# Mean squares of the heads summed along the free axis, the last square sum on VectorE, and the first normalisation dealt out anew over three engines

## The chip, the cores and the metric

The kernel runs on one core of a Trainium2 chip. The core has five engines with their own instruction queues: TensorE (PE; its weight loads are listed apart as PEld), VectorE (DVE), ScalarE (ACT), GpSimd (POOL) and SyncE (SP), which here only issues DMAs. The metric is the device time of one execution in microseconds; the median of several runs counts. Everything is FP32 in and out.

## The reference, cut to what matters

One layer of an encoder on 512 tokens of 1024 channels:

```python
h = rms_norm(x, norm1_g)                      # mean of squares over the 1024 channels
proj = h @ w_in                               # pool, attention, recurrence, gates
y_attn: o = (softmax(s1) - lam * softmax(s2)) @ v        # 4 heads of 128 channels
        o = rms_norm(o, gain) * 0.8                      # over the 128 channels of a head
y_rec:  o = o_forward + o_backward                       # 4 heads of 128 channels
        o = rms_norm(o, gain) * silu(g)
merged = sum of gate * (y @ w_up); x = x + merged @ w_out
x = x + (silu(h2 @ w_a) * (h2 @ w_b)) @ w_ffn_out        # h2 = rms_norm(x, norm2_g)
return rms_norm(x, final_norm_g)
```

So there are eight head norms over 128 channels each (four of attention, four of the recurrence), a first norm, a second norm and a final norm over 1024 channels.

## The kernel before

**Layout.** Most activations lie transposed: channels on the 128 partitions, the 512 tokens along the free axis (four blocks of 128, `NB = 4`). A product is made exact enough by splitting both sides into a rounded part and a remainder (`_hi`, `_lo`, type FP32R) and adding three products hi x hi, hi x lo, lo x hi. ScalarE makes the rounded part of a weight (`whi`, L191), VectorE the remainder (`wlo`, L192), 128x1024 at a time. Small products inside the heads are plain FP32.

**Order of the work.** TensorE's order is the program's: `mm` (L96) and `transpose` (L104) pin it. It is made when the kernel is built, by a small planner (`Pipe`): heads and a stream of weight jobs are Python generators; each `yield ("w", t, slack)` says that the head's next piece should stand at least t us of planned TensorE time later, with up to `slack` of putting off so that small pieces of several heads come together; `yield ("e", name, t)` waits for a named event. The other engines' order is set by the framework from a simulated timeline, except where the program pins one instruction behind another (`behind`, `issue_after`). Every queue runs in order, so an instruction that waits holds up those behind it on its engine.

**Head norms** (`head_norm`, L692 to L717). A head's output is in PSUM, 128 channels by 512 tokens. ScalarE squares it (`sqo`, L697) and copies it times the gain (`og`, L698). TensorE sums over the partitions by four FP32 products with `onesD` (a column of 1/128), one per token block: the result is a 128x4 tile, tokens on the partitions. VectorE adds epsilon (for attention it first multiplies twice by the softmax denominators' reciprocal `rr`), GpSimd takes the power -1/2 (`rso`, L147), and TensorE spreads the result again over the channels by four transposes of a broadcast column. VectorE then multiplies `og` with it. In the recurrence `og` is also multiplied with the silu gate (L1013, L1014); `rec_scan` and `att_head` call the helper at L1011 and L1158.

**Front** (L558 to L689, written out by hand). The blocks of x arrive by SyncE's queue in the order x, x, weights rq, weights rf, x, x, weights rb. For each of four token blocks `norm_rows` squares 1024 columns on ScalarE with an accumulated sum, GpSimd adds epsilon and takes the power, VectorE makes two 512-wide products with the row factor and the gain (which stands spread over the partitions in two PSUM banks, `g_ps`; for blocks 2 and 3 ScalarE first copies it to `g_b`). `rows_T` transposes the rows on TensorE, ScalarE casts the result (`hT_hi`, L515), VectorE makes its remainder (`hT_lo`, L519). Eleven products of no use (`probe`) keep TensorE running before that. Then three weight tiles take their first products with token blocks 0 and 1 (`turns`), the transposes of blocks 2 and 3 between them.

**Tail** (`seven_job`, the last of the output products). Token blocks 2 and 3 come last. For the last block ScalarE squares columns 512 to 1023, 0 to 255 and 256 to 511 into three accumulators (`out_sums`, L1479), VectorE adds the three (`out_rstd`, L1495), GpSimd takes the power, ScalarE scales one half of the columns and VectorE the other, and each half is stored by the queue of ScalarE or of SyncE (`out_store`, L1503 to L1506).

Of the kernel before, what the change touches and what calls it, by code (L numbers as in the profile page):

```python
# [11 lines left out]
F32 = mybir.dt.float32  # L12
# [6 lines left out]
P = 128  # L19
# [63 lines left out]
def encoder_kernel(ctx: ExitStack, tc: tile.TileContext, x, norm1_g, w_in, pool_w, pool_scale,  # L83
# [48 lines left out]
    onesD, minus1 = fixed[:, 0:1], fixed[:, 1:2]  # L132
    nc.vector.memset(onesD, 1.0 / P)
# [15 lines left out]
    def rsqrt_eps(dst, mean):  # L149

        ms = small.tile([P, 8], F32, name="ms")[:, :mean.shape[1]]
        eng = nc.vector if mean.space == PSUM else nc.gpsimd
        eng.tensor_scalar(out=ms, in0=mean, scalar1=1.0, scalar2=EPS, op0=ALU.mult, op1=ALU.add)  # L153
        return pow_mhalf(dst, ms)
# [335 lines left out]
    def norm_rows(src, g_b, work, after=()):  # L490
        sq = work.tile([P, D], F32, name="hrow")
        ss = small.tile([P, 1], F32, name="ss")
        with behind(after):
            on_act = nc.scalar.activation(out=sq, in_=src, func=AF.Square, scale=D ** -0.5, accum_out=ss).ins
        rstd = small.tile([P, 1], F32, name="rstd")
        rsqrt_eps(rstd, ss)
        h = work.tile([P, D], F32, name="hrow")
        for half in range(2):
            cs = slice(half * 512, half * 512 + 512)
            g = g_b[half] if isinstance(g_b, list) else g_b[:, cs]  # L500
            with behind(after):
                on_dve = nc.vector.scalar_tensor_tensor(out=h[:, cs], in0=src[:, cs], scalar=rstd, in1=g,  # L502
                                                        op0=ALU.mult, op1=ALU.mult).ins
        return h, on_dve, on_act
# [44 lines left out]
    g_b = xg.tile([P, D], F32, name="g1b")  # L549
# [9 lines left out]
    for name in ("x", "x", "rq", "rf", "x", "x", "rb"):  # L559
        if name == "x":  # L560
            t, src = xp.tile([P, D], F32, name="xin"), xblk[len(xt)]
            xt.append(t)
# [32 lines left out]
    nc.vector.tensor_copy(out=g_cols, in_=gt[:, 0:KT])  # L595
# [10 lines left out]
    for _ in range(11):  # L606
# [7 lines left out]
    def first_split(after):  # L614
        f = First()
        with behind(after):
            f.hi, f.lo = split_w(first_raw[len(first)], KT, P, None, 64)
        first.append(f)
        return LAST["whi"], LAST["wlo"]

    h0, on_dve, on_act = norm_rows(xt[0], g_ps, xw)
    h1, on_dve, on_act = norm_rows(xt[1], g_ps, xw, (on_act, on_dve))
    last = first_split((on_act, on_dve))
    for h, b, where in ((h0, 0, ("tp", "tp")), (h1, 1, ("rc", "mm"))):
        for half in range(2):
            with behind(last):
                on_act = rows_T(h, hT, b, half, None, where[half])
            last = on_act, LAST["hT_lo"]
    on_act, on_dve = first_split(last)
    for half in range(2):  # L630
        with tc.issue_after(on_act):
            on_act = nc.scalar.copy(out=g_b[:, half * 512:half * 512 + 512], in_=g_ps[half]).ins
    last = on_act, on_dve
    h2, on_dve, on_act = norm_rows(xt[2], g_b, xw, last)
    h3, on_dve, on_act = norm_rows(xt[3], g_b, xw, (on_act, on_dve))
    last = first_split((on_act, on_dve))
# [44 lines left out]
    turns(0, 4)  # L681
    turns(1, 8)
# [9 lines left out]
    def head_norm(o_ps, tmp, gain, r0=None, bufs=2, slack=0.0):  # L692
# [3 lines left out]
        sq = tmp.tile([P, S], F32, name="sqo", bufs=bufs)  # L696
        nc.scalar.activation(out=sq, in_=o_ps, func=AF.Square)  # L697
        nc.scalar.activation(out=og, in_=o_ps, func=AF.Copy, scale=gain)  # L698
        yield ("w", 1.3, slack)
        sp = bank("tp")  # L700
# [1196 lines left out]
```

## Time and profile before

| what | value |
|---|---|
| median of 3 runs | 871.75 us (871.43 to 872.48) |
| the profiled execution's own time | 871.81 us |
| its span, first to last instruction | 870.0 us |
| busy: TensorE, VectorE, ScalarE, GpSimd | 862.4, 659.2, 448.7, 37.1 us |
| DMA | 87.54 MB, 101 GB/s in the mean |

A timeline row gives start, length, engine, line, operation, output<-inputs, shapes, and how many like instructions follow each other; in brackets stands how long the engine had been idle before and what ended that. A row of a tile's or a line's instructions gives shortest, median and longest duration in ns and the first and last start in us. A row of windows gives the stretch, then for TensorE, its weight loads, VectorE, ScalarE and GpSimd the busy us and the number of instructions, then the granted clock, the DMA share and GB/s. A page row of waits gives the waiting engine and line, what it waited for, and total, number and longest in us.

### The profile page before, as it was taken

Reading aid. Unit: us, or ns where it says so; the run is one execution under the profiler, and the core shown is the slowest. Engines: PE = TensorE matmul, PEld = TensorE weight load, DVE = VectorE, ACT = ScalarE, POOL = GpSimd, SP = SyncE. Lnnn points to the kernel's source line nnn. Section 1 sums busy time; section 2 is a strip of 40 time slices with the busy share of each in tenths; the row PEclk is TensorE's granted clock in tenths of the full one; section 3 lists DMA queues with packets and bytes.
Section 4 is the critical chain, followed back from the end, with each engine's and each line's share of the span. In section 5 each row is a group of like instructions: output and inputs, shape, how many; then the busy total and the mean of one; then the engine's idle time right before and its main releaser. Section 6 shows DMA issues by size and latency. Waiting matters only on the chain.

```text
span 870.0 us, 14113 instructions
## 1 busy us (share of the span) xinstructions
PE 862.4 (99%) x5713; PEld 786.1 (90%) x5713; DVE 659.2 (76%) x979; ACT 448.7 (52%) x721; POOL 37.1 (4%) x83
## 2 busy tenths in 40 slices
PE   9999999999999999999999999999999999999997
PEld 8989998888988888899999998999999999988886
DVE  6779644845757888987776756988888888847996
ACT  6644343435757664563354425655555655533563
POOL 2000000000102220000000001000000000000001
PEclk9999999999999999999999999999999999999999
DMA  8330113024133321343332840344433433355002
GB/s 245 98 122 25 50 49 121 25 74 151 43 95 90 90 68 49 97 146 98 97 98 97 288 124 1 85 112 128 114 98 108 136 98 99 121 194 192 2 1 98
DMA packets 115694, 87.54 MB, mean 101 GB/s; under 512 B 3862, under 2 KB 104748, under 8 KB 115628
## 3 DMA queue, kind: packets, MB, share of 16 engines
q1 hardware_dynamic: 115036, 85.57, 32.2%
q8 instruction: 45, 0.74, 0.4%
q10 hardware_dynamic: 592, 1.05, 0.3%
q14 instruction: 21, 0.17, 0.1%
HBM read 84.52 MB, written 2.10 MB: 100 GB/s over the span
## 4 chain that ended last, share of the span: by engine, by line
PE 98%; issue 1%; DMA 0%; DVE 0%; POOL 0%; ACT 0%; POOLq 0%
PE mm L96 65%; PE rc L96 28%; PE tp L96 3%; PE tp L104 2%; DMA xin<-in_x_dram 0%; PE rc L104 0%; DVE hrow L502 0%; POOL rstd L147 0%; ACT silu L1479 0%; ACT x L1503 0%; DVE x L1472 0%; DVE x L1481 0%; PE mm L104 0%; POOLq L1892 0%; POOL ms L153 0%
## 5 line engine op out<-in xcount | busy, mean ns | idle before, releaser
L191 ACT CAST whi<-raw 128x1024 fp32r<-128x1024 f32 (+1 forms) x134 | 127.5, 959 | 140.7 <-PE mm L96 95.2
L192 DVE TENSOR_TENSOR wlo<-raw,whi 128x1024 fp32r<-128x1024 f32 (+1 forms) x134 | 147.8, 1106 | 50.9 <-ACT whi L191 41.3
L96 PE MATMUL mm<-hT_hi,whi 128*128 128x512 f32 (+1 forms) x344 | 81.3, 370 | 0.0
L96 PE MATMUL mm<-hT_hi,wlo 128*128 128x512 f32 (+1 forms) x344 | 80.0, 368 | 0.0
L96 PE MATMUL mm<-hT_lo,whi 128*128 128x512 f32 (+1 forms) x344 | 78.8, 367 | 0.0
L96 PEld LDWEIGHTS mm<-hT_hi,whi 128*128 128x128 f32 x344 | 59.2, 188 | 10.3 <-ACT hT_hi L515 0.2
L96 PEld LDWEIGHTS mm<-hT_lo,whi 128*128 128x128 f32 x344 | 59.1, 188 | 9.8
L96 PEld LDWEIGHTS mm<-hT_hi,wlo 128*128 128x128 f32 x344 | 58.8, 188 | 9.5
L318 DVE TENSOR_TENSOR slo<-sums,shi 128x1024 fp32r<-128x1024 f32 x54 | 65.7, 1217 | 0.0
L316 ACT CAST shi<-sums 128x1024 fp32r<-128x1024 f32 x54 | 56.8, 1052 | 4.1 <-DVE sums L280 3.3
L276 DVE TENSOR_TENSOR sums<-raw 128x1024 f32<-128x1024 f32 x27 | 32.9, 1218 | 1.2 <-DMA raw<-in_w_in_dram 1.2
L96 PE MATMUL mm<-y_arena,whi 128*128 128x512 f32 x128 | 32.7, 394 | 0.0
L96 PE MATMUL mm<-whi,y_arena 128*128 128x256 f32 (+1 forms) x192 | 32.1, 317 | 0.0
L96 PE MATMUL rc<-kq,kc 128*128 128x128 f32 x224 | 30.4, 284 | 0.0
L96 PEld LDWEIGHTS rc<-kq,kc 128*128 128x128 f32 x224 | 29.2, 191 | 1.1
L961 DVE TENSOR_TENSOR kq<-kq,pyr 128x256 f32<-128x256 f32 x48 | 18.2, 420 | 15.8 <-PE rc L96 15.8
L96 PEld LDWEIGHTS mm<-whi,y_arena 128*128 128x128 f32 x192 | 27.9, 189 | 2.6
L929 ACT COPY kc<-kq 128x512 f32<-128x512 f32 x28 | 18.6, 667 | 21.6 <-DVE kq L955 8.2
L1114 ACT ACTIVATE s<-s,mx 128x512 f32<-128x512 f32 x32 | 23.0, 719 | 10.9 <-DVE mx L1112 10.2
L96 PEld LDWEIGHTS mm<-y_arena,whi 128*128 128x128 f32 x128 | 23.7, 188 | 5.1
L1413 DVE TENSOR_TENSOR g<-mm,g 128x256 f32<-128x256 f32 x21 | 8.9, 424 | 23.9 <-PE mm L96 23.4
L96 PE MATMUL mm<-fhi,shi 128*128 128x256 f32 x168 | 25.9, 276 | 0.0
(409 smaller groups left out, 2053.5 us busy)
## 6 DMA issues: line engine op xcount, KB each, us to landing
raw<-in_w_in_dram SPq DMA_DIRECT2D x44, 512.0 KB, 4.2
raw<-in_w_ffn_in_dram SPq DMA_DIRECT2D x44, 512.0 KB, 4.1
raw<-in_w_in_dram SPq DMA_DIRECT2D x8, 1024.0 KB, 5.2
raw<-in_w_ffn_out_dram SPq DMA_DIRECT2D x7, 1024.0 KB, 4.8
raw<-in_w_out_dram SPq DMA_DIRECT2D x4, 1024.0 KB, 10.1
xin<-in_x_dram SPq DMA_DIRECT2D x4, 512.0 KB, 4.6
raw<-in_w_up_rec_dram SPq DMA_DIRECT2D x2, 1024.0 KB, 7.6
raw<-in_w_up_pool_dram SPq DMA_DIRECT2D x2, 1024.0 KB, 5.0
```

The costliest lines, as they stand in the source:

```text
L96: i = nc.tensor.matmul(out_, lhsT=lhsT, rhs=rhs, start=start, stop=stop, skip_group_check=chain)
L104: tc.keep_in_program_order(nc.tensor.transpose(out_, in_, idn))
L191: LAST["whi"] = nc.scalar.copy(out=hi, in_=view).ins
L192: LAST["wlo"] = nc.vector.tensor_tensor(out=lo, in0=view, in1=hi.bitcast(F32), op=ALU.subtract).ins
L276: nc.vector.tensor_tensor(out=strided(sums, 0, [[2 * half, 2], [1, half]]), in0=strided(self.raw, 0, [[3 * half, 2], [1, half]]), in1=stri ...
L316: nc.scalar.copy(out=hi, in_=view)
L318: on_dve = nc.vector.tensor_tensor(out=lo, in0=view, in1=hi.bitcast(F32), op=ALU.subtract).ins
L929: nc.scalar.copy(out=strided(kc, 0, [[2 * n, S // (2 * n)], [n, 2], [1, n]]), in_=strided(kq, 2 * S, [[2 * n, S // (2 * n)], [S + n, 2], [ ...
L961: nc.vector.tensor_tensor(out=xv, in0=xv, in1=tv, op=ALU.mult)
L1114: nc.scalar.activation(out=s, in_=s, func=AF.Exp, scale=-1.0, bias=mx[:, c:c + 1], accum_out=zz[:, i, c:c + 1])
L1413: on_dve = nc.vector.tensor_tensor(out=c["g"], in0=c["x"], in1=c["g"], op=ALU.add).ins
```

## The change

**Heads.** The recurrence's output products swap their operands, so that the result has tokens on the partitions and channels along the free axis. Its squares (ScalarE) are summed along the free axis by VectorE (`token_sums`), VectorE adds epsilon, GpSimd takes the power, VectorE scales the rows, and four transposes on TensorE turn them; one VectorE instruction then applies gain and silu gate. Attention heads 0 to 2 copy their output to SBUF, transpose it by four transposes, sum the squares of that in the same way, and keep the transposes that spread the result. The last attention head keeps the products with a column, now of ones. Attention's small steps go from VectorE to GpSimd. The planner's waits change: 4.6 in the recurrence, 4.8 and 3.5 in attention, where one of 1.3 and one of 3.55 stood.

**Front.** The squares of blocks 0 and 1 are shared between ScalarE (512 and 768 columns) and VectorE; blocks 2 and 3 carry epsilon as a 1025th column, and use the gain from PSUM. The remainders of the first two weights are halved between VectorE and GpSimd; one of the first four casts goes to VectorE; the first weight's cast stands behind the first cast of rows. Five warm-up products in place of eleven, and the turns of the first two weights alternate.

**Tail.** The last square sum is one VectorE instruction that starts from the sum of the others; the columns 0 to 511 of the last block are scaled and stored in two halves; one addition of block 3 is made earlier.

```diff
-    onesD, minus1 = fixed[:, 0:1], fixed[:, 1:2]
-    nc.vector.memset(onesD, 1.0 / P)
+    ones, minus1 = fixed[:, 0:1], fixed[:, 1:2]
+    nc.vector.memset(ones, 1.0)
...
+    def row_rstd(src, work, after=(), on_act=D):
...
+            last = (nc.scalar.activation(out=sq[:, a], in_=src[:, a], func=AF.Square, scale=D ** -0.5,
+                                         accum_out=ss[:, 0:1]).ins,)
+            if on_act < D:
+                last += (nc.vector.tensor_tensor_reduce(out=sq[:, b], in0=src[:, b], in1=src[:, b], scale=1.0 / D,
+                                                        scalar=EPS, op0=ALU.mult, op1=ALU.add,
+                                                        accum_out=ss[:, 1:2]).ins,)
+        if on_act < D:
+            nc.gpsimd.tensor_tensor(out=ss[:, 2:3], in0=ss[:, 0:1], in1=ss[:, 1:2], op=ALU.add)
+            pow_mhalf(rstd, ss[:, 2:3])
...
-    for _ in range(11):
+    for _ in range(5):
         mm(ps[:, 0:256], probe[:, 32:32 + P], probe[:, 0:256], True, True)
...
+        shared = len(first) < 2
+        view, n = first_raw[len(first)], KT // 2 if shared else KT
...
+        if shared:
+            nc.gpsimd.tensor_tensor(out=f.lo[:, n:], in0=view[:, n:], in1=f.hi[:, n:].bitcast(F32), op=ALU.subtract)
...
+    r0, (act, dve) = row_rstd(xt[0], xw, (on_dve,), 512)
+    r1, (act, dve) = row_rstd(xt[1], xw, (act, dve), 768)
+    h0, on_dve = scaled_rows(xt[0], r0, g_ps, xw, (dve,))
+    h1, on_dve = scaled_rows(xt[1], r1, g_ps, xw, on_dve)
+    t00, t01 = (turned(h0, half, "tp") for half in range(2))
+    t10, t11 = (turned(h1, half, where) for half, where in enumerate(("rc", "mm")))
+    on_act = cast(t00, 0, 0, nc.scalar.copy, (act,))
+    on_dve = cast(t01, 0, 1, nc.vector.tensor_copy, on_dve)
+    on_act, on_dve = first_split(on_act, on_dve)
+    on_act = cast(t10, 1, 0, nc.scalar.copy, on_act)
+    on_act = cast(t11, 1, 1, nc.scalar.copy, on_act)
...
-    turns(0, 4)
-    turns(1, 8)
+    for i in (0, 1, 0, 1):
+        turns(i, 2)
+    turns(1, 4)
...
+    def token_sums(o, tmp, bufs=2):
+        sq = tmp.tile([P, NB, P], F32, name="sqo", bufs=bufs)
+        ss = small.tile([P, NB], F32, name="mo")
+        nc.scalar.activation(out=sq, in_=o, func=AF.Square)
+        nc.vector.tensor_reduce(out=ss, in_=sq, op=ALU.add, axis=mybir.AxisListType.X)
...
+            if last:
+                mm(turned[:, 0, b:b + 1], sq[:, bs], ones, True, True)
+            else:
+                transpose(turned[:, b, :], og[:, bs], ident)
...
-            mm(o, vs[b], pt[:, b, :], True, False)
+            mm(o, pt[:, b, :], vs[b], True, False)
...
-        og, rbp = yield from head_norm(ps, rt, gain_r, slack=slack)
+        o = rt.tile([P, NB, P], F32, name="og")
+        sums = token_sums(ps, rt)
+        nc.scalar.copy(out=o, in_=ps)
+        r = small.tile([P, NB, 1], F32, name="rso")
+        rsqrt_eps(r[:, :, 0], sums, P)
+        nc.vector.tensor_tensor(out=o, in0=o, in1=r.to_broadcast([P, NB, P]), op=ALU.mult)
+        yield ("w", 4.6, slack)
+        turned = bank("tp")
+        for b in range(NB):
+            transpose(turned[:, b * P:(b + 1) * P], o[:, b, :], ident)
...
+        out_add(3, 256, x[1][:, 256:], ALU.subtract)
         sv_product(x[0], 7, 0, False, True)
...
-        out_sums(3, 256, 256, 2, src[:, second])
-        out_store(3, out_rstd(3, 3)[0], src)
+        nc.vector.tensor_tensor_reduce(out=junk[:, 0:256], in0=x3, in1=x3, scale=1.0 / D, scalar=total,
+                                       op0=ALU.mult, op1=ALU.add, accum_out=whole)
...
+        nc.scalar.dma_start(out=outb[3][:, 512:], in_=a)
+        nc.vector.tensor_scalar(out=src[:, first], in0=src[:, first], scalar1=rstd, scalar2=None, op0=ALU.mult)
+        nc.sync.dma_start(out=outb[3][:, first], in_=src[:, first])
+        nc.vector.scalar_tensor_tensor(out=src[:, second], in0=x3, scalar=rstd, in1=FF["g"][:, second],
+                                       op0=ALU.mult, op1=ALU.mult)
+        nc.sync.dma_start(out=outb[3][:, second], in_=src[:, second])
```

More of the change, by code (lines that the diff above doesn't have):

```diff
@@ L487, in rows_mm, with scaled_rows @@
                     yield
[L490 to L497 removed]
+    def row_rstd(src, work, after=(), on_act=D):
+        sq = work.tile([P, src.shape[1]], F32, name="hrow")
+        ss = small.tile([P, 4], F32, name="ss")
+        a, b = slice(0, on_act), slice(on_act, D)
+        rstd = small.tile([P, 1], F32, name="rstd")
+        with behind(after):
+            last = (nc.scalar.activation(out=sq[:, a], in_=src[:, a], func=AF.Square, scale=D ** -0.5,
[7 more added lines that the diff above has]
+            pow_mhalf(rstd, ss[:, 2:3])
+        elif on_act > D:
+            pow_mhalf(rstd, ss[:, 0:1])
+        else:
+            rsqrt_eps(rstd, ss[:, 0:1])
+        return rstd, last
+    def scaled_rows(src, rstd, g_b, work, after=()):
+        h = work.tile([P, src.shape[1]], F32, name="hrow")
         for half in range(2):
@@ L612, in encoder_kernel, with first_split @@
     first = []
-    def first_split(after):
+    def first_split(act, dve):
         f = First()
-        with behind(after):
[L617 to L628, printed above, removed]
@@ new lines, in first_split @@
+        f.hi, f.lo = (wsp.tile([P, 1088], F32R, name=name)[:, 16:1040].rearrange("p (k c) -> p k c", k=KT)
+                      for name in ("whi", "wlo"))
+        with behind(act):
+            on_act = (nc.scalar.copy(out=f.hi, in_=view).ins,)
+        if shared:
+            nc.gpsimd.tensor_tensor(out=f.lo[:, n:], in0=view[:, n:], in1=f.hi[:, n:].bitcast(F32), op=ALU.subtract)
+        with behind(dve):
+            on_dve = (nc.vector.tensor_tensor(out=f.lo[:, :n], in0=view[:, :n], in1=f.hi[:, :n].bitcast(F32),
+                                              op=ALU.subtract).ins,)
@@ new lines, in first_split, with turned, place, cast @@
+        first.append(f)
+        return on_act, on_dve
+    def turned(h, half, where):
+        pt = bank(where, (P, 4, P))
+        for j in range(4):
+            c = half * 4 + j
+            transpose(pt[:, j, :], h[:, c * P:(c + 1) * P], ident)
+        return pt
+    def place(t, b, half):
+        return t[:, half * 4:half * 4 + 4, b * P:(b + 1) * P]
+    def cast(pt, b, half, eng, after):
+        with behind(after):
+            return (eng(out=place(hT[0], b, half), in_=pt).ins,)
+    def rest(pt, b, half, eng, after):
+        with behind(after):
+            return (eng.tensor_tensor(out=place(hT[1], b, half), in0=pt, in1=place(hT[0], b, half).bitcast(F32),
+                                      op=ALU.subtract).ins,)
```

126 lines of the change are left out of this document (69 added, 57 removed).

## The prediction

> **What bounds the kernel now.** I read the page's first lines, its chain that ended last, TensorE's waits, and then only the places that the diff touches.
>
> ```profile
> PE 862.4 (99%) x5713; PEld 786.1 (90%) x5713; DVE 659.2 (76%) x979; ACT 448.7 (52%) x721; POOL 37.1 (4%) x83
> PE 98%; issue 1%; DMA 0%; DVE 0%; POOL 0%; ACT 0%; POOLq 0%
> PE mm L96 <- POOL ident masks.py:199: 1.3, 1, 1.3
> ```
>
> The chain is TensorE for 98% of the span. The last line is the whole answer of TensorE's waits: past the wait for the identity at the start nothing is listed. A busy TensorE alone would prove little, but a TensorE that never waits means that time taken out of its stream is time off the end, as long as the other engines still deliver. So I count TensorE's stream first, and then what might make it wait. The profiled execution took 871.81 us, 0.06 above the median of 871.75; I count from 871.8 and call both the same.
>
> **Heads: what leaves TensorE.** Each of the eight heads now gets its mean squares from four FP32 products with a one-column right side, and then four transposes that spread the result over the partitions.
>
> ```profile
> L96 PE MATMUL tp<-fixed,sqo x64: 164/250/250, 124.6 to 331.7; 128*128 128x1 f32 x64
> 195.13 0.94 PE L96 MATMUL tp<-fixed,sqo 128*128 128x1 f32 x8
> 195.94 1.19 PE L96 MATMUL mm<-hT_hi,wlo 128*128 128x512 f32 x4
> 196.97 2.00 PE L96 MATMUL mm<-hT_hi,whi 128*128 128x512 f32 x8
> 198.81 1.52 PE L96 MATMUL mm<-hT_lo,whi 128*128 128x512 f32 x6
> 200.16 0.60 PE L104 MATMUL tp<-ident,rso 128*128 128x128 f32 x4
> 200.52 0.71 PE L96 MATMUL mm<-hT_lo,whi 128*128 128x512 f32 x2
> 16.06 1.03 PE L104 MATMUL tp<-ident,hrow 128*128 128x128 f32 x8
> ```
>
> Durations overlap, so the cost is read from start to start. An FP32 product makes two records (64 for 8 x 4), a transpose one. Four products hold TensorE from 195.13 to 195.94, 0.81 us; four transposes from 200.16 to 200.52, 0.36. A group also delays what follows: the four products behind it need 1.03 (195.94 to 196.97), where the eight undisturbed ones behind them need 1.84 (196.97 to 198.81), 0.92 for four: an interruption costs about 0.1.
>
> Recurrence heads (four). The diff swaps the operands of the output products, so that rows are tokens; their number and 128x128 shape stay, at no cost. The squares are then summed along the free axis, so the four one-column products go (4 x 0.81 = 3.24), and the four transposes of the spread rstd become four transposes of the scaled output: one for one, 0. One interruption per head goes too where it stood alone, two of them: 0.2. Together 3.4.
>
> Attention heads 0 to 2. The products give way to four transposes of the output, and the four spreading transposes stay: 3 x (0.81 - 0.36) = 1.35. Head 3 keeps its products (ones instead of 1/128). Were a data transpose dearer than a spreading one, the bound is the front's row at 16.06: eight in 1.03, less the last one's own 0.27, over seven steps, 0.11 each, so 0.44 for four; 0.08 less gain per head, 0.6 on seven heads.
>
> **Heads: what the other engines get.** Per recurrence head VectorE keeps two 512-wide products (0.69; the gain now rides on the gate's) and gains a reduction of 128x512, which the trace does not show. The nearest rows, a one-input 512-wide operation (0.49, L1505 below) and the fused one with its accumulator read (0.68 + 0.08), bound it; I take 0.68.
>
> ```profile
> L1112 DVE CUSTOM_DVE_ANT_0 s<-strip,rc x32: 677/683/689, 216.0 to 317.3; 128x512 f32<-128x512 f32 x32
> L147 POOL TENSOR_TENSOR rso<-ms,mhalf x4: 1006/1009/1015, 126.0 to 196.4; 128x4 f32<-128x4 f32 x4
> L697 ACT ACTIVATE sqo<-rc x8: 575/597/599, 123.5 to 329.4; 128x512 f32<-128x512 f32 x8
> L1014 DVE TENSOR_TENSOR og<-og,tp x4: 680/688/689, 130.6 to 200.8; 128x512 f32<-128x512 f32 x4
> 125.00:130.00 5.00, 5.00 (x46) 5.00 (x47) 1.46 (x6) 1.24 (x3) 1.01 (x1) 1.00 0.00 0
> 130.00:135.00 5.00, 5.00 (x35) 4.48 (x33) 2.47 (x5) 2.50 (x4) 1.98 (x2) 1.00 0.00 0
> ```
>
> The new chain from the last output product to the transposes is square 0.60, reduction 0.68, epsilon 0.16, power 1.01, scaling 0.69: 3.14, with five hand-overs of 0.08 (the step from 865.11 to 865.19 in the tail below) 3.5. The planner gives it 4.6. The third and fourth figures of the two windows are VectorE and ScalarE: at most 2.5 of 5 us busy, so room of 1.1 for queueing should do. What stands behind those transposes on TensorE is the job stream's products; each us too late would be a us of the end. I take no wait.
>
> For attention the chain is square 0.60, reduction 0.68, three small GpSimd steps at about 0.2, power 1.01 and six hand-overs, 0.5: 3.4, where the planner now gives 4.8. Queueing is heavier here:
>
> ```profile
> 265.96 0.16 DVE L712 TENSOR_TENSOR rso<-rso,rr 128x4 f32<-128x4 f32 x1
> 266.38 1.61 POOL L1121 TENSOR_TENSOR co<-zz,fixed 128x1 f32<-128x1 f32 x1 [0.30 <-ACT s L1114]
> 261.57 0.95 PE L96 MATMUL tp<-fixed,sqo 128*128 128x1 f32 x8
> 267.50 0.60 PE L104 MATMUL tp<-ident,rso 128*128 128x128 f32 x4
> ```
>
> In head 0 the old chain ran from the sums' end (262.4) to 266.12, 3.7 us for four VectorE steps of 0.16 and a power, 1.65 us of work: 2.1 of queueing. With as much, the new one needs 5.5. But the planner sets the spreading transposes beside a score group of the next head, here 5.1 us behind the sums where the old wait was 3.55, so I take the full 1.35. The other bound is 0.7 (5.5 - 4.8) of waiting in each of three heads: 2.1 back.
>
> **Front.** Its order is written out by hand. TensorE's first real product starts at 10.09.
>
> ```profile
> 4.44 1.06 ACT L494 ACTIVATE hrow<-xin 128x1024 f32<-128x1024 f32 x1 [0.67 <-DMA xin<-in_x_dram]
> 4.51 0.17 DVE L595 COPY g1c<-tp 128x8 f32<-128x8 f32 x1 [3.56 <-PE tp L104]
> 5.80 1.06 ACT L494 ACTIVATE hrow<-xin 128x1024 f32<-128x1024 f32 x1 [0.21 <-DMA xin<-in_x_dram]
> 5.93 1.56 PE L96 MATMUL mm<-probe 128*128 128x256 f32 x11
> 5.95 0.56 POOL L147 TENSOR_TENSOR rstd<-ms,mhalf 128x1 f32<-128x1 f32 x1
> 6.54 2.77 DVE L502 SCALAR_TENSOR_TENSOR hrow<-xin,rstd,rc 128x512 f32<-128x512 f32 x4 [1.87 <-POOL rstd L147]
> 7.35 1.31 PE L104 MATMUL tp<-ident,hrow 128*128 128x128 f32 x8
> 10.12 0.59 ACT L515 CAST hT_hi<-mm 128x512 fp32r<-128x512 f32 x1
> L153 POOL TENSOR_SCALAR ms<-ss x8: 190/190/689, 5.7 to 541.7; 128x1 f32<-128x1 f32 x8
> ```
>
> Block 0: ScalarE squares 512 of 1024 columns (0.63, between 0.42 for 256 in the tail and 1.06), VectorE the rest from 4.60 for 0.68, done at 5.28. GpSimd adds (0.23) and starts its power at 5.68 instead of 5.95: 0.27 earlier. Block 1: 768 columns to 6.74, addition, power from 7.13; VectorE takes it up at about 7.7 instead of 7.9. The last transposes and the last cast (10.12 now) come 0.2 to 0.25 earlier, and with them the first products. On ScalarE the weight cast now stands behind the first cast of the transposed rows; by these rows (0.48 a cast, 0.95 the weights, from 7.77) it frees ScalarE at 9.20, in time for the third. The six warm-up products taken away (0.12 each) ran while TensorE would have waited for the rows at 7.35: 0, and five still end before 7.1. The interleaved turns and the later blocks only take up results that are ready earlier.
>
> The dear part is GpSimd's half of the first weight remainder, 128x512 from about 9.3, which TensorE wants near 11.45. No row shows it; GpSimd's 128x128 clearing and selecting took 0.2 to 0.3, so 0.5 to 1.6 by width and two inputs, and a GpSimd operation beside VectorE stretches (0.19 to 0.69 in L153, 0.55 to 1.61 above), so it ends between 9.8 and 12.0: up to 0.55 late. Behind it on GpSimd stands only the next half and the late blocks' powers. The front is worth between -0.25 and +0.3; I take -0.2, since most of that interval is in time.
>
> By the Trainium skill (GPSIMD Engine Reference, section 3.1) a two-input elementwise operation costs about 2.6 cycles an element, 1.1 us at 1.2 GHz as an estimate; by that it would be in time and the front would give its full 0.25.
>
> **Tail.**
>
> ```profile
> 863.90 0.42 DVE L1472 TENSOR_TENSOR x<-x,tp 128x256 f32<-128x256 f32 x1 [0.59 <-PE tp L96]
> 864.35 0.42 ACT L1479 ACTIVATE silu<-x 128x256 f32<-128x256 f32 x1 [0.63 <-DVE x L1472]
> 864.89 0.22 DVE L1495 SCALAR_TENSOR_TENSOR ss<-stats 128x1 f32<-128x1 f32 x1
> 865.19 0.55 POOL L147 TENSOR_TENSOR rstd<-ss,mhalf 128x1 f32<-128x1 f32 x1 [2.74 <-DVE ss L1495]
> 865.78 0.49 DVE L1505 TENSOR_SCALAR x<-u,rstd 128x512 f32<-128x512 f32 x1 [0.66 <-POOL rstd L147]
> 866.53 0.34 ACTq L1504 DMA_DIRECT2D out_dram<-x  x1
> ```
>
> From 864.35 on, square, accumulator read and sum become one VectorE reduction of 256 columns: 0.42 with its read, done at 864.77, power at 864.85 instead of 865.19: 0.34. ScalarE's store follows, 866.19 instead of 866.53. On SyncE two stores of half the width take the place of one; the second is issued behind 0.35 + 0.42 of VectorE work, at about 866.2, not behind ScalarE's. The moved addition falls into VectorE's idle time before 859.6; without that cover it would cost its old place's 0.42, which TensorE's last products hide. Term 0.3, bounds 0 (if the two stores land as late as before) and 0.5.
>
> **Sum.** 3.4 + 1.35 + 0.2 + 0.3 = 5.25, so 871.8 - 5.3 = 866.5.
>
> **The rivals.** (1) Attention's chain arrives late: 2.1 comes back, 868.6. For: the queueing above; against: the distances the planner left. (2) The front's clock falls. Twelve cold products took 2.93 us and the clock rose about 4 us after the first; if TensorE fell back, some 4 us at half pace would cost 2.0: 868.5. Now
>
> ```profile
> 868.00:869.00 1.00, 0.00 (x0) 0.00 (x0) 0.00 (x0) 0.00 (x0) 0.00 (x0) 0.99 0.49 191
> 869.00:870.00 1.00, 0.00 (x0) 0.00 (x0) 0.00 (x0) 0.00 (x0) 0.00 (x0) 0.50 0.00 0
> 1.34 2.93 PE L96 MATMUL mm<-ident 128*128 128x128 f32 x12 [1.34 <-POOL ident masks.py:199]
> ```
>
> the granted clock fell 5 us after the last product's addition began (863.9 to 869), whereas between the shortened warm-up (6.53) and the first product (9.84) lie 3.3 us with sixteen transposes. The Trainium skill (TensorE: Matmul & The Clock Gate, Part 4) says that transposes do not count as busy and that an idle window of 3.4 us suffices (Part 1); by that rule 3.3 is just short of it, where 2.8 was safe. (3) Slower: the new link through VectorE and the square behind the transposes sit behind a 1.22 us weight split in every head, and TensorE waits. It decides from 5.3 / 7 = 0.76 us a head; at 1.0 it is 7 - 5.3 = 1.7 slower, 873.5. For: splits run all the time; against: the half-idle windows above. (4) The freed TensorE time goes nowhere, because VectorE bounds what comes behind:
>
> ```profile
> 345.00:365.00 20.00, 20.00 (x90) 16.46 (x89) 19.12 (x24) 11.90 (x17) 0.00 (x0) 1.00 0.39 106
> ```
>
> VectorE is 19.12 of 20 busy there. If TensorE then waits for what it gained before, only the tail is left: 871.5. Against: that work depends on TensorE's earlier results and should start earlier with them.
>
> **How the numbers follow.** Forecast 0.68, (1) 0.16, (2) with a late GpSimd half 0.07, (3) 0.05, (4) 0.04. The forecast's own bounds are 865.5 (more interruptions saved, a faster tail, the full front) and 867.7 (dear transposes 0.6, front +0.3, no tail gain); with (1) and (2) the range ends at 868.9. About 0.2%, 1.7 us, is what can be told from no change: (4) is "same", (3) slower, the rest faster.
>
> **What would show it.** Right: no one-column products but head 3's four (8 records), no new line in TensorE's waits, first product near 9.85, the last power 1.0 us after the last addition began. Wrong: TensorE waiting for the scaled output, for the spread rstd or for the first weight remainder, or products at half pace near 10 us.

## The result, and the profile after

The changed kernel took 866.89 us in the median of 4 runs (866.52 to 867.39), the kernel before 871.79 in 4 runs beside it: a ratio of 0.9943, with a 95% interval from 0.9926 to 0.9960. The prediction was 866.5, in a range from 865.5 to 868.9. Run again later beside another set of runs of before (871.58), the changed kernel took 866.53 (866.46 to 866.85), a ratio of 0.9941 (0.9929 to 0.9954).

First the page of the kernel after: the span, the busy times and the chain of work that ended last; then the whole answer of TensorE's waits.

```profile
span 865.1 us, 14041 instructions
...
PE 857.3 (99%) x5663; PEld 780.2 (90%) x5663; DVE 663.0 (77%) x980; ACT 446.4 (52%) x716; POOL 41.3 (5%) x99
...
PE 98%; DMA 1%; DVE 0%; ACT 0%; POOL 0%; POOLq 0%; issue 0%; DVEq 0%; SPq 0%
```

```profile
PE mm L96 <- POOL ident masks.py:199: 1.3, 1, 1.3
PE tp L104 <- DVE hrow L519: 0.3, 1, 0.3
PE rc L104 <- DVE hrow L519: 0.2, 1, 0.2
```

TensorE is still the chain for 98% of the span, with 50 records fewer (5713 before) and 5.1 us less busy time (862.4 before), and the span is 4.9 us shorter. VectorE took on 3.8 us and ScalarE gave up 2.3, and neither moved the end. The two new waits are in the front, for scaled rows before the first product, where the prediction's sign of no new line fails in this execution; the second one lists neither. Behind the front none is listed; a short delay behind a late weight load shows only in the starts of the products (experiment 11 has one). The lines that the prediction named for the heads stand in the tiles of the squares and of the outputs (shortest, median and longest in ns, then the first and the last start in us):

```profile
L96 PE MATMUL tp<-fixed,sqo x8: 168/250/250, 326.3 to 327.0; 128*128 128x1 f32 x8
...
L750 DVE TENSOR_REDUCE mo<-sqo x7: 674/685/687, 124.2 to 309.1; 128x4 f32<-128x512 f32 x7
```

```profile
L104 PE MATMUL tp<-ident,og x28: 270/272/276, 128.3 to 307.5; 128*128 128x128 f32 x28
```

Of the 64 one-column records 8 are left, those of attention head 3. Seven heads transpose their output instead (7 x 4 = 28), and the reduction that no row of before showed takes 0.685 us, where the prediction took 0.68.

To see where the time went, I set the start of the same product on TensorE in one trace against its start in the trace of before. Each row is one product, named by its start in the kernel before; the other columns say how much earlier (-) or later (+) it starts, in us. The last row is the difference of the spans.

```
start before   after  after,  heads:  heads:  front   tail    no      columns
               .      again   rec.    att.    alone   alone   front   back
 10.09         -0.15  -0.22   +0.17   +0.48   +0.15   +0.19   +0.24   -0.14
 12.28         +0.06  +0.04   +0.04   +0.26   +0.32   +0.21   +0.24   +0.05
 16.85         +0.06  -0.10   -0.05   +0.12   +0.18   +0.07   +0.50   -0.09
117.97         +0.06  -0.10   -0.05   -0.17   +0.17   -0.21   +0.19   -0.10
222.03         -3.54  -3.70   -3.69   -0.17   +0.19   -0.22   -3.45   -0.33
359.95         -4.67  -5.13   -3.69   -1.52   +0.18   -0.23   -4.80   -1.69
863.34         -4.67  -5.13   -4.17   -1.86   +0.19   -0.24   -5.31   -1.68
span           -4.90  -5.37   -4.2    -1.8    +0.2    -0.4    -5.5    -1.9
```

(The last column is experiment 5, which puts one-column products back; the others are named below. Differences of 0.1 to 0.6 that arise between 12.28 and 31 us and between 490 and 541 us are mostly the pace of the last section.) Read down the first column: the front brings nothing (+0.06), the four recurrence heads 3.60, the attention heads 1.13, the long stretch from 360 to 863 neither gives nor takes, and the tail brings 0.23. In the second execution of the same kernel the recurrence heads bring the same 3.60, the attention heads 1.43 and the tail 0.24.

Two stretches show how the heads look now. The first is recurrence head 3 in the timeline of the kernel after, the answer to the rows at 195 to 200 us that the prediction showed.

```profile
194.83 0.68 DVE L1085 TENSOR_TENSOR og<-og,rso 128x512 f32<-128x512 f32 x1
...
195.63 0.43 PEld L104 LDWEIGHTS tp<-ident,og 128*128 128x128 f32 x4 [0.19 <-issue]
195.70 0.60 PE L104 MATMUL tp<-ident,og 128*128 128x128 f32 x4
...
196.05 1.64 PE L96 MATMUL mm<-hT_lo,whi 128*128 128x512 f32 x6
```

The four transposes hold TensorE from 195.70 to 196.05, 0.35 us, as the spreading ones did, and the 0.81 of the sums is gone. The scaled output is ready at 195.51, 0.12 before the load for its transposes begins: the planner's distance of 4.6 suffices, but with little to spare. The second stretch is attention head 0, the one whose queueing the prediction feared.

```profile
258.03 0.60 PE L104 MATMUL tp<-ident,og 128*128 128x128 f32 x4
...
258.82 0.60 ACT L749 ACTIVATE sqo<-tp 128x512 f32<-128x512 f32 x1
...
260.22 0.68 DVE L750 TENSOR_REDUCE mo<-sqo 128x4 f32<-128x512 f32 x1
...
260.98 0.20 POOL L777 TENSOR_TENSOR mo<-mo 128x4 f32<-128x4 f32 x1 [1.77 <-DVE mo L750]
...
261.55 1.02 POOL L147 TENSOR_TENSOR rso<-mo,mhalf 128x4 f32<-128x4 f32 x1
...
262.41 1.23 DVE L192 TENSOR_TENSOR wlo<-raw,whi 128x1024 fp32r<-128x1024 f32 x1 [0.30 <-ACT s L1192]
262.53 1.16 POOL L1198 TENSOR_TENSOR co<-zz,nlam 128x1 f32<-128x1 f32 x1
...
263.64 0.20 POOL L781 TENSOR_TENSOR rso<-rso,rr 128x4 f32<-128x4 f32 x1
...
263.89 0.42 PEld L104 LDWEIGHTS tp<-ident,rso 128*128 128x128 f32 x4
```

From the end of the transposes (258.63) to the spread rstd (263.84) the chain takes 5.2 us: 0.8 of waiting for VectorE before the reduction and 1.1 on GpSimd between the power and the last product. That 1.1 is a single small step of attention (L1198). It took 0.19 at 256.88, and 1.16 here beside VectorE's weight split (L192): the two engines hold each other up, as experiment 6 shows. The load of the spreading transposes starts 0.05 behind the spread rstd. It was just in time, and no wait is recorded.

### The profile page after: what moved, and what is told of

It reads as the page before. It is cut to its first block, busy times and chain, and to the rows that moved or that the text cites. A ratio compares the mean times of both kernels' runs of the same rounds, so it can differ in the third digit from the quotient of the medians.

```text
span 865.1 us, 14041 instructions
## 1 busy us (share of the span) xinstructions
PE 857.3 (99%) x5663; PEld 780.2 (90%) x5663; DVE 663.0 (77%) x980; ACT 446.4 (52%) x716; POOL 41.3 (5%) x99
## 4 chain that ended last, share of the span: by engine, by line
PE 98%; DMA 1%; DVE 0%; ACT 0%; POOL 0%; POOLq 0%; issue 0%; DVEq 0%; SPq 0%
PE mm L96 65%; PE rc L96 28%; PE tp L96 2%; PE tp L104 2%; DMA xin<-in_x_dram 1%; PE rc L104 0%; ACT hrow L498 0%; DVE hrow L519 0%; PE mm L104 0%; POOLq L1980 0%; POOL rstd L147 0%; DVE silu L1831 0%; DVE x L1550 0%; DVEq L1980 0%; SPq L588 0%
## 5 line engine op out<-in xcount | busy, mean ns | idle before, releaser
L191 ACT CAST whi<-raw 128x1024 fp32r<-128x1024 f32 (+1 forms) x131 | 124.3, 957 | 130.3 <-PE mm L96 84.0
L192 DVE TENSOR_TENSOR wlo<-raw,whi 128x1024 fp32r<-128x1024 f32 (+1 forms) x131 | 144.1, 1102 | 54.5 <-ACT whi L191 36.9
```

The source lines that it names most:

```text
L191: LAST["whi"] = nc.scalar.copy(out=hi, in_=view).ins
L192: LAST["wlo"] = nc.vector.tensor_tensor(out=lo, in0=view, in1=hi.bitcast(F32), op=ALU.subtract).ins
```

## The experiments

All times are medians; each ratio is against the kernel before, run in turn with it on the same chip. The changed kernel's own ratio is 0.9943 and, again, 0.9941.

**1 to 4: one part alone.** Each of these kernels is the one before with one part of the change: the recurrence heads, attention heads 0 to 2, the front, or the tail.

```diff
 # heads of the recurrence alone; attention keeps its one-column products
-            o = ps[:, b * P:(b + 1) * P]
-            mm(o, vs[b], pt[:, b, :], True, False)
+            o = ps[:, b, :]
+            mm(o, pt[:, b, :], vs[b], True, False)
...
+        sums = token_sums(ps, rt)
```

> Only the recurrence heads of the change, all else as before. Theory (the gain is TensorE time that leaves the stream): in the trace of after, products behind the recurrence stand 3.60 us earlier than those in front of it (from 0.06 later at 118 to 3.54 earlier at 223), so 871.8 - 3.6 = 868.2, with no new line in TensorE's waits. Rival (the parts help each other: the heads' gain needs the new front or attention to be delivered): less than 2.5 us, above 869.3.

Measured: 867.92 (867.19 to 868.33), ratio 0.9957 (0.9942 to 0.9971). The table's third column has 3.64 across the four heads, and TensorE's waits show no new line. The theory holds.

```diff
 # attention heads 0 to 2 alone; the recurrence keeps its one-column products
-        og, rbp = yield from head_norm(ps, at, gain_a, rr, 1, 6.0 if h < HEADS - 1 else 0.0)
+        og, rbp = yield from head_norm(ps, at, rr, 4.8 if h < HEADS - 1 else 3.5, 1, 6.0 if h < HEADS - 1 else 0.0, h == HEADS - 1)
```

> Only the attention heads of the change. Theory: three heads at 0.45 and no more, less what TensorE then waits for; after showed 0.24 of waiting in front of a head's value product at 270.9, so 1.15 to 1.4: 870.4 to 870.65. Rival (the wait comes from attention's longer chain itself, not from where things happen to fall): the same 0.24 is missing here too, 870.65. If the whole 1.4 is there, the wait belongs to the order that the whole change gives.

Measured: 870.43 (869.97 to 871.58), ratio 0.9987 (0.9978 to 0.9996). Between 222 and 360 us the products gain 1.35, the prediction's term to the hundredth.

```diff
 # the front alone
-    h0, on_dve, on_act = norm_rows(xt[0], g_ps, xw)
-    h1, on_dve, on_act = norm_rows(xt[1], g_ps, xw, (on_act, on_dve))
...
+    r0, (act, dve) = row_rstd(xt[0], xw, (on_dve,), 512)
+    r1, (act, dve) = row_rstd(xt[1], xw, (act, dve), 768)
...
-    for _ in range(11):
+    for _ in range(5):
```

> Only the front of the change. Theory from the trace of after: nothing won, 0.06 later behind it, because the first x block landed 0.13 later and VectorE's half of the first weight remainder took 1.52 us beside GpSimd's: 871.8 to 871.9. Rival (the prediction's step: 0.2 won, hidden in after by a late transfer that is chance): 871.6, with the first product at 9.85.

Measured: 871.76 (870.84 to 871.99), ratio 1.0001 (0.9991 to 1.0011). The front alone is worth nothing that can be told; its products stand 0.17 later from 31 us on, in an execution in which the second block of x was taken up only at 6.23 us (5.80 before).

```diff
 # the tail alone
-        out_sums(3, 256, 256, 2, src[:, second])
-        out_store(3, out_rstd(3, 3)[0], src)
+        nc.vector.tensor_tensor_reduce(out=junk[:, 0:256], in0=x3, in1=x3, scale=1.0 / D, scalar=total,
+                                       op0=ALU.mult, op1=ALU.add, accum_out=whole)
...
+        nc.sync.dma_start(out=outb[3][:, first], in_=src[:, first])
...
+        nc.sync.dma_start(out=outb[3][:, second], in_=src[:, second])
```

> Only the tail of the change. Theory from the trace of after: the power starts 1.09 us after the last addition instead of 1.30, and the second half-width store lands last and gives part of it back: 0.2 won, 871.6. Rival (the prediction's step): 0.34 won, 871.45.

Measured: 871.37 (871.02 to 871.70), ratio 0.9996 (0.9987 to 1.0005), too little to be told from nothing by the time. Its trace has the theory's 0.2: the power starts 1.09 us behind the last addition, and the tail gains 0.23 (the last two rows of the table). Against the kernels before them, the four parts come to -3.62, -1.11, +0.22 and -0.17, together -4.7; the whole change measured -4.9 and -5.05. The parts add up to within 0.4 us. By the times alone, whose intervals reach 0.8 us or more to either side, no more can be said; by the traces the recurrence heads bring 3.64 alone and 3.60 in the whole change, the attention heads 1.35 and 1.13 or 1.43, the tail 0.23 and 0.23 or 0.24.

**5: one-column products put back.** If the gain at the recurrence heads is TensorE's time and nothing else, useless work of the same kind must cost it again.

```diff
         turned = bank("tp")
+        for b in range(NB):
+            mm(turned[:, b:b + 1], o[:, b, :], ones, True, True)
         for b in range(NB):
             transpose(turned[:, b * P:(b + 1) * P], o[:, b, :], ident)
```

> The changed kernel, with four FP32 products with a one-column right side put back into each of the four recurrence heads, right before the four transposes of the scaled output; the transposes overwrite what they give, so they are extra work whose result nobody uses, and nothing waits for them but TensorE's own order. Theory (the recurrence heads' gain is TensorE's time for the one-column products, 0.81 us a head): 4 x 0.81 = 3.25 slower than the changed kernel, 866.9 + 3.25 = 870.1, all of it at the four heads. Rival (the gain came from something else in the new order, such as the shorter chain through GpSimd or fewer interruptions, and TensorE has time to spare there): within 0.5 of 866.9.

Measured: 869.91 (869.54 to 871.10), ratio 0.9981 (0.9972 to 0.9990), 3.0 to 3.4 us slower than the changed kernel's two medians. In the table the four heads keep 0.23 of the 3.60, so the products cost 3.37, 0.84 a head. The timeline of this kernel shows one of them:

```profile
198.05 0.99 PE L96 MATMUL tp<-fixed,og 128*128 128x1 f32 x8
...
198.91 0.63 PE L104 MATMUL tp<-ident,og 128*128 128x128 f32 x4
...
199.29 0.94 PE L96 MATMUL mm<-hT_lo,whi 128*128 128x512 f32 x3
```

Four products with one column hold TensorE for 0.86 us here (198.05 to 198.91), more than twice as long as four whole 128x128 transposes (0.38, to 199.29). The rival is out: TensorE has no time to spare at the heads, and the new chain through VectorE and ScalarE is hidden.

**6: the first weight remainders whole on VectorE.** In the kernel after, the front's row that the prediction had priced at 0.68 took 1.52 (the timelines of the front are shown with this experiment).

```diff
-        shared = len(first) < 2
+        shared = False
```

> The changed kernel, with the first two weight remainders whole on VectorE instead of half on GpSimd. Theory (VectorE and GpSimd hold each other up: VectorE's half beside GpSimd's took 1.52 us where 0.68 is its time alone): the whole remainder on VectorE takes about 1.25 and ends no later than the two halves do now; the time stays within 0.3 of 866.9, at most 0.2 better. Rival (sharing is worth its half, 0.6 us of VectorE in the front for each of two): 0.5 or more slower, 867.4 to 868.

Measured: 866.45 (866.20 to 867.81), ratio 0.9943 (0.9930 to 0.9955): 0.44 under the changed kernel's first median and 0.08 under its second, so not told apart from it by the time, though the expectation had at most 0.2 better. The timeline of the changed kernel, then of this one:

```profile
9.40 1.29 POOL L642 TENSOR_TENSOR wlo<-raw,whi 128x512 fp32r<-128x512 f32 x1 [1.64 <-ACT whi L640]
...
9.73 1.52 DVE L644 TENSOR_TENSOR wlo<-raw,whi 128x512 fp32r<-128x512 f32 x1
...
11.17 0.68 DVE L665 TENSOR_TENSOR hT_lo<-tp,hT_hi 128x512 fp32r<-128x512 f32 x1
```

```profile
9.77 1.22 DVE L644 TENSOR_TENSOR wlo<-raw,whi 128x1024 fp32r<-128x1024 f32 x1
...
10.90 0.68 DVE L665 TENSOR_TENSOR hT_lo<-tp,hT_hi 128x512 fp32r<-128x512 f32 x1
```

Two engines need 1.85 us for what VectorE alone does in 1.22 (9.40 to 11.25 against 9.77 to 10.99), and VectorE is free for the next step 0.27 earlier without its helper. Sharing was not a division of labour.

The kernel with eleven warm-up products (experiment 10) and the changed kernel run again (11) show how the two engines hold each other up. First the one, then the other:

```profile
9.96 0.69 DVE L644 TENSOR_TENSOR wlo<-raw,whi 128x512 fp32r<-128x512 f32 x1
10.01 1.80 POOL L642 TENSOR_TENSOR wlo<-raw,whi 128x512 fp32r<-128x512 f32 x1 [2.19 <-ACT whi L640]
```

```profile
9.41 1.28 POOL L642 TENSOR_TENSOR wlo<-raw,whi 128x512 fp32r<-128x512 f32 x1 [1.84 <-ACT whi L640]
9.55 1.69 DVE L644 TENSOR_TENSOR wlo<-raw,whi 128x512 fp32r<-128x512 f32 x1
```

Whichever starts first takes its own time, and the other takes nearly as much longer as the first still runs. Where VectorE started 0.05 ahead it needed 0.69 and GpSimd 1.80; where GpSimd started ahead it needed 1.28, and VectorE's half ended at 11.24 or 11.25, whether it had begun at 9.55 or at 9.73: 0.55 behind GpSimd's end (10.69) both times. The Trainium skill (SBUF — State Buffer, section "Who interferes with whom") says that a VectorE instruction with two SBUF inputs contends with a GpSimd instruction that reads SBUF, that the port pair the two share is under "an exclusive lock", and that "Issue order, not op shape, decides who blocks." The trace agrees, with 1.52 to 1.69 for 0.68, but for 0.13 us: VectorE's half ends 0.55 behind GpSimd's, less than its own 0.68.

**7: attention head 3 also turned.** The prediction left head 3 aside, since the change keeps its products; is that head worth 0.45 as well? The edit also gives its spreading transposes the planner's distance of the other heads, 4.8 instead of 3.5.

```diff
-        og, rbp = yield from head_norm(ps, at, rr, 4.8 if h < HEADS - 1 else 3.5, 1, 6.0 if h < HEADS - 1 else 0.0, h == HEADS - 1)
+        og, rbp = yield from head_norm(ps, at, rr, 4.8, 1, 6.0 if h < HEADS - 1 else 0.0, False)
```

> The changed kernel, with attention head 3 handled like heads 0 to 2: its output transposed and summed along the free axis instead of four one-column products. Theory (0.81 - 0.36 of TensorE a head, as in heads 0 to 2): 0.45 faster, 866.45. Rival (head 3's chain is the one that the attention output waits for; the summing along the free axis puts a square, a reduction and their hand-overs behind the transposes, some 1 us more, and TensorE has nothing left to fill it): 0.3 to 1 slower, with a new line in TensorE's waits near 330 us.

Measured: 867.72 (867.52 to 868.05), ratio 0.9955 (0.9942 to 0.9967), 0.8 to 1.2 slower than the changed kernel's medians. TensorE's waits of this kernel have the line that the rival named, and the timeline shows it:

```profile
PE tp L104 <- POOL rso L781: 1.4, 1, 1.4
```

```profile
326.30 0.60 PE L104 MATMUL tp<-ident,og 128*128 128x128 f32 x4
...
327.57 0.69 DVE L750 TENSOR_REDUCE mo<-sqo 128x4 f32<-128x512 f32 x1 [2.65 <-ACT sqo L749]
328.40 0.20 POOL L777 TENSOR_TENSOR mo<-mo 128x4 f32<-128x4 f32 x1 [11.33 <-DVE mo L750]
...
329.32 1.23 DVE L192 TENSOR_TENSOR wlo<-raw,whi 128x1024 fp32r<-128x1024 f32 x1 [1.06 <-PE mm L96]
330.06 0.54 POOL L781 TENSOR_TENSOR rso<-rso,rr 128x4 f32<-128x4 f32 x1
...
330.66 0.65 PE L104 MATMUL tp<-ident,rso 128*128 128x128 f32 x4 [1.43 <-POOL rso L781]
```

The theory was wrong and the rival right. The four products cost TensorE 0.45 more than four transposes, but the chain behind them is short: in the changed kernel GpSimd begins head 3's chain at 327.59, here at 328.40, with square and reduction in between. What stands in front of the spreading transposes at this head ends 1.43 us before they can start, and TensorE stands for that long. Of this 0.34 is again a GpSimd step beside VectorE's weight split (L781, 0.54 instead of 0.20). The larger planner distance put no more products in between: the same ten stand there in both kernels. The same swap gains 0.45 where the stream has work enough to put in front of the chain, and loses about 1 where it has too little.

**8: one store for the last block's first half.** In the changed kernel the two half stores on SyncE's queue left at 861.29 and 861.71, with the last power at 860.32.

```diff
-        nc.sync.dma_start(out=outb[3][:, first], in_=src[:, first])
...
-        nc.sync.dma_start(out=outb[3][:, second], in_=src[:, second])
+        nc.sync.dma_start(out=outb[3][:, 0:512], in_=src)
```

> The changed kernel, with the last block's columns 0 to 511 stored by one transfer behind both scalings instead of two of half the width. Theory (the second of two half stores on one queue landed last, 3.86 us behind the power where the store of ScalarE alone had taken 3.82 with a later start): one store, issued at the second's time, lands no later, 0 to 0.25 faster, 866.65 to 866.9, with the last power still 1.09 us behind the last addition. Rival (the store's size sets its landing time): 0.1 to 0.3 slower.

Measured: 867.09 (866.59 to 867.12), ratio 0.9945 (0.9933 to 0.9958). By the time this isn't told from the changed kernel, but the traces differ. The tail of the changed kernel, then the last rows with one store:

```profile
859.23 0.42 DVE L1550 TENSOR_TENSOR x<-x,tp 128x256 f32<-128x256 f32 x1 [0.81 <-PE tp L96]
859.68 0.48 DVE L1831 CUSTOM_DVE_ANT_0 silu<-x,stats 128x256 f32<-128x256 f32 x1
860.09 0.08 DVE L1831 DVE_READ_ACCUMULATOR2_ANT stats<- 128x1 f32 x1
860.32 0.55 POOL L147 TENSOR_TENSOR rstd<-stats,mhalf 128x1 f32<-128x1 f32 x1 [2.53 <-DVE stats L1831]
...
861.71 0.38 SPq L1842 DMA_DIRECT2D out_dram<-u  x1
```

```profile
860.08 0.55 POOL L147 TENSOR_TENSOR rstd<-stats,mhalf 128x1 f32<-128x1 f32 x1 [2.54 <-DVE stats L1831]
...
861.41 0.37 ACTq L1837 DMA_DIRECT2D out_dram<-x  x1
861.43 0.33 SPq L1841 DMA_DIRECT2D out_dram<-u  x1
```

From the last power to the end of the span, the changed kernel takes 4.81 us (865.13 - 860.32) and this one 5.26 (865.34 - 860.08), although its store leaves at nearly the same distance from the power (1.35 against 1.39). So with two full-size transfers leaving together the end comes 0.45 later, the rival's way. It is no scatter: all eight traces with the two half stores take 4.80 to 4.82. Size alone doesn't explain it, since the kernel before also stores two full halves and takes 4.84; but its first store leaves 1.10 behind the power and the first half store of the changed kernel 0.97, where here none leaves before 1.33. That an early first store is what counts fits all three, but no run varied it alone. The split is worth those 0.45: the tail of this kernel loses 0.23 (its products are 4.92 ahead of before's at 863.34, its span 4.69), where the changed kernel's gains 0.23.

**9: everything but the front.** The changed heads and tail, with the front of before.

```diff
 # the changed kernel, but the front as it was
+    h0, on_dve, on_act = norm_rows(xt[0], g_ps, xw)
...
-    r0, (act, dve) = row_rstd(xt[0], xw, (on_dve,), 512)
...
-    for _ in range(5):
+    for _ in range(11):
```

> The changed kernel with the front of the kernel before: heads and tail changed, front not. Theory (the front's new order wins nothing by the time TensorE's stream is dense): within 0.3 of the changed kernel, so 866.6 to 867.2, and the same products start within 0.15 of the changed kernel's from 20 us on, as far as the pitch of the products is the same in both. Rival (the front is worth the 0.2 to 0.25 of the prediction, and chance hid it): 867.1 to 867.4, with 0.2 at 20 us and behind.

Measured: 866.31 (866.11 to 867.59), ratio 0.9941 (0.9928 to 0.9953): at least as fast as with the new front (866.53 in the same rounds), and below the theory's 866.6 to 867.2. Its products aren't within 0.15 of the changed kernel's at 20 us (+0.48 against +0.06), though they are at 31 us (+0.18). In the profiled execution its products are 0.19 later than before's from 31 us on, with x taken up 0.29 later; that is the scatter of this front in four kernels that keep it, from -0.21 to +0.19 at 118 us. The kernels with the new front and shared halves lie between -0.10 and +0.17. The front can't be told from nothing.

**10: eleven warm-up products again.**

```diff
-    for _ in range(5):
+    for _ in range(11):
```

> The changed kernel with eleven warm-up products again instead of five. Theory (the six products ran while TensorE would have waited for the rows, and the clock holds without them): the first transposes of rows may start up to 0.3 later, the first product within 0.1 of 9.94, the time within 0.2 of 866.9. Rival (the shorter warm-up costs clock in the first products): 0.3 or more faster.

Measured: 866.59 (866.11 to 867.30), ratio 0.9943 (0.9930 to 0.9957). That is 0.31 under the 866.9 of the expectation, where the rival would put it; but the changed kernel itself took 866.53 in the same rounds, 0.06 less, so the eleven gain nothing, and the clock needed no more warm-up: the rival is out. The place is not as expected: the first product comes at 10.47, not within 0.1 of 9.94, since the longer warm-up pushes the first transposes of rows from 7.10 to 7.76 and with them the casts behind. Of that half microsecond 0.1 is left at the product of 12.28 (+0.16 in this kernel, +0.06 in the changed one), because in both the products before it wait for VectorE and ScalarE; by the times even that 0.1 can't be seen.

**11: the changed kernel once more.**

> The changed kernel, unchanged, once more: how far the same products move between executions of one program. Theory (two things in the profiles are chance: the wait of 0.24 near 270.6, and whether a 256-wide product of the first 30 us takes 0.118 or 0.113): the wait may be there or not, the products between 12 and 30 us may stand up to 0.5 earlier, and the median is 866.6 to 867.1. Rival (both belong to the kernel): the same products within 0.05 of the first profile throughout, with the wait at 270.6.

Measured: 866.53 (866.46 to 866.85), given above and 0.07 under the expected range. The products between 12.28 and 31 us stand 0.03 to 0.17 earlier, and the wait near 270.6 is not there. The rows of the first profile and then of this one:

```profile
270.27 0.59 ACT L1210 CAST aT_hi<-tp 128x512 fp32r<-128x512 f32 x1
...
270.56 0.39 PE L96 MATMUL rc<-l,q 128*128 128x512 f32 x1
270.91 1.20 PE L96 MATMUL rc<-aT_hi,va_hi 128*128 128x512 f32 x4
```

```profile
269.85 0.59 ACT L1210 CAST aT_hi<-tp 128x512 fp32r<-128x512 f32 x1
...
270.39 0.39 PE L96 MATMUL rc<-l,q 128*128 128x512 f32 x1
...
270.62 1.07 PE L96 MATMUL rc<-aT_hi,va_hi 128*128 128x512 f32 x4
```

In the first profile the value product starts 0.35 behind the product ahead of it, in the second 0.23, which is its pace: ScalarE's cast, queued behind others, comes just in time or just late. With the value products behind it, slowed as well (1.20 for four instead of 1.07), that is the 0.3 by which the attention heads differ between the two executions (1.13 against 1.43). No other place of the heads separates the two executions, so it is chance and not part of the change.

## Why the prediction was right, point by point

**What bounds the kernel.** Right: time taken from TensorE's stream came off the end, unabated from 360 us to the last product (-4.67 at both). Of the signs that were to show it, 8 one-column records came out; the first product at 9.94 and the last power at 1.09 are 0.1 behind theirs, and the waits in the front are two new lines in the first execution.

**Recurrence heads, 3.4 predicted, 3.60 measured**, and 3.60 to 3.64 in all eight traces that have this part without products put back. The four one-column products were 0.84 a head and not 0.81 (experiment 5: 3.37); the rest, 0.23, has the size of the two interruptions that the prediction put at 0.2, though no run separates them. That the swapped operands and the transposes of the scaled output cost nothing holds.

**Attention heads, 1.35 predicted, 1.35 alone and 1.43 in the second execution**, 1.13 in the first with its chance wait. A data transpose is no dearer than a spreading one (0.35 for four); the bound of 0.6 for that didn't arise. Rival (1), the late chain, was close: 5.2 us of chain in head 0, with 0.05 to spare, where the prediction counted 3.4 of work: 0.8 went to waiting for VectorE and 1.1 to GpSimd beside it. Experiment 7 shows what it looks like where it happens.

**Front, -0.2 predicted, nothing measured: the step that failed.** Up to the first product the working was right. Experiment 8, whose front is the changed one, took up the second block of x at the same time as the kernel before (5.81 and 5.80), and its first product starts 0.22 earlier, at 9.87. But its first product with a weight remainder starts at 11.28, where before had 11.34, and from 12.28 on it is 0.05 later. The row of the kernel before, then those of experiment 8:

```profile
11.34 1.11 PE L96 MATMUL mm<-hT_hi,wlo 128*128 128x256 f32 x8
```

```profile
9.87 1.42 PE L96 MATMUL mm<-hT_hi,whi 128*128 128x256 f32 x8
...
11.28 0.86 PE L96 MATMUL mm<-hT_hi,wlo 128*128 128x256 f32 x5
```

The prediction let VectorE's half stand at its own length, and asked only whether GpSimd's would be stretched to 12.0. It is the other way round: GpSimd's half starts first and is done at 10.69, and VectorE's waits for it, 1.52 to 1.69 for 0.68. The rows shown (GpSimd 0.19 to 0.69, 0.55 to 1.61) had the mechanism but not that either engine can be the one held up. Two things show that the halves set the place. In five executions with halves and five warm-up products (the changed kernel twice, experiments 5, 7 and 8) the second block was taken up between 5.73 and 5.94, and yet the product of 12.28 stands at +0.04 to +0.07 in all (experiment 3, with the block at 6.23, has +0.32). And without the halves (experiment 6) it stands at -0.09, although the block came at 5.97.

By the Trainium skill (SBUF — State Buffer, section "Who interferes with whom"), taken as a full lock, VectorE's half ends at GpSimd's end plus its own time, an estimate of 10.69 + 0.68 = 11.37 (11.25 measured), past the 11.34 at which before's remainder product starts, and the front's term would have been about 0. By the Trainium skill (GPSIMD Engine Reference, section 3.1) the prediction's estimate for GpSimd's half was 1.1 us; it took 1.29, in time as that sentence has it, but VectorE's half was not.

**Rival (2), the clock.** It did not happen: the granted clock stays at 1.00 behind the front, and eleven warm-up products gain nothing. How long a gap it would have taken, no run shows.

**Tail, 0.3 predicted, 0.23 measured; the mechanism right, one term mis-sized.** The prediction had 0.34 from the power. The fused reduction took 0.48 and a read of 0.08, the hand-over to GpSimd 0.15, so the power starts 1.09 behind the start of the last addition, where before it was 1.29 (865.19 - 863.90): 0.20. From the power to the end nothing changes (4.84 before, 870.03 - 865.19, and 4.81 after), although SyncE's last store now leaves 1.39 behind the power and not 1.10: the half store ahead of it makes up for the second scaling (without it the end comes 0.45 later, experiment 8).

**Rivals (3) and (4).** Neither: no wait for the new chain in any head but the one of experiment 7, and behind 360 us TensorE keeps every hundredth although VectorE is busy nearly all the time there. The sum as measured is 3.60 + 1.35 + 0 + 0.23 = 5.2, against 5.25 predicted. It takes each part where chance disturbed it least; the whole change gave 4.90 and 5.05 by the medians. That the front's missing 0.2 and the recurrence heads' surplus of 0.2 cancel is luck.

## What to carry to other kernels

Where the chain of waits is one engine and its list of waits is empty, price a change by that engine's start-to-start times and let the other engines count only by whether they still arrive; this came within 0.4 us of 4.9. Four products with one column cost TensorE more here than four whole 128x128 transposes (0.81 to 0.86 us against 0.35 to 0.38), so summing on another engine paid, where there was other work to put in front of the longer chain. And before work is split between VectorE and GpSimd, check whether both halves read two inputs from SBUF: here such halves ran one after the other, and even a GpSimd step of 0.19 us took 1.16 beside such a step of VectorE.

## What the runs showed that I had not expected

The pace of the products is not the same in every execution, with the granted clock at 1.00 throughout. Nearly the same stretch of the same work in the changed kernel and then in the kernel of experiment 6 (each row has TensorE's busy time and number of products first, and the granted clock third from the end):

```profile
22.00:29.00 7.00, 7.00 (x62) 7.00 (x61) 3.13 (x7) 4.63 (x6) 0.00 (x0) 1.00 0.26 76
```

```profile
22.00:29.00 7.00, 7.00 (x64) 7.00 (x63) 3.65 (x9) 4.97 (x6) 0.00 (x0) 1.00 0.27 80
```

More products fit into the same time in one execution than in another. In such stretches the median from the start of one product of 256 columns to the start of the next is 0.113 us in one trace and 0.118 in the other. That moved the same products by up to 0.6 us: by 0.14 between 12.28 and 16.85 us, where only before, the changed kernel and experiment 8 of all the traces run at 0.118; from -0.23 at 17 us to -0.52 at 31 us against before in experiment 6; and by another 0.5 and 0.6 between 490 and 541 us in the kernels with the recurrence heads alone and without the front (the -4.17 and -5.31 of the table). It is as much as the front and the tail of this change together, and all but 0.09 of experiment 6's lead at 31 us is of this kind and no gain of its edit. What decides the pace stays open; no run here varied it on purpose.
